# A layer's prologue with its loads in another order and its first projections on half the tokens

## The chip, the cores and the metric

The kernel runs on one core of a Trainium2 chip. The metric is the device time of one execution in microseconds; the times shown are of three runs. Beside them stands one profiled execution with its trace, in which every instruction of every engine has a start and a duration.

Engines are named as in the trace: PE (TensorE) with its weight loads PEld, DVE (VectorE), ACT (ScalarE), POOL (GpSimd), and SP, whose queue SPq issues all the DMA loads.

## What is computed

One layer of a flow-matching backbone, over 1024 latent tokens and 256 context tokens of width 1024. The part that the change touches is the beginning:

```python
m_lat = jnp.split(jax.nn.silu(c) @ w_mod + b_mod, 6, axis=-1)
h_lat = modulate(rms_norm(x_lat, norm_mix_pre), m_lat[0], m_lat[1])   # h * (1 + scale) + shift
q, k, v, r, lr, z, xbc, dt_raw = jnp.split(h_lat @ w_in, PROJ_SPLITS, axis=-1)
```

Behind it come the convolution of `xbc`, two bidirectional scans (gated linear attention and a state-space scan), the output projection and a SwiGLU block. They are the same before and after.

## The kernel before

Products are made in three fp16 parts: `split_w` makes of a weight block a high half on ACT (line 213) and a lower half on DVE (line 214), `mod_split` does the same for activations (lines 381 to 383), and `mm3` issues high times high, high times low and low times high (lines 219 to 221).

The first stage makes three 128-column blocks of the projection (`m` = 4, 5, 0, the ones that feed the convolution) for all latent tokens. The tokens are two halves of 512, the contraction has eight steps `k` of 128 channels, so there are 3 x 2 x 8 products of three matmuls. Their six accumulators `accs` fill the six PSUM buffers of the tag `ps` while the stage lasts. Two more PSUM buffers, tag `pf` (`psum_f`), serve whatever runs beside.

The stage needs

- x in eight tiles of 128 tokens (`load_x(t)`, t = 2 to 9, 512 KB each, line 363). `norms` squares and sums a pair of tiles (one on ACT, line 374, one on DVE, line 372), makes the reciprocal root (`rstd_act`, lines 194 to 199) and scales both tiles on DVE (line 377). `x_T(k, g, pool)` transposes channel block k of the four tiles of half g on PE (line 413) and copies the result out of PSUM, on ACT for even k and DVE for odd k (line 414).
- shift and scale of each channel. `mod_load(j)` loads two pieces of 256 columns of w_mod, 1 MB each (line 332; `wm`, four buffers), piece 1 for the scale and piece 0 for the shift; together they serve k = 2j and 2j + 1. `mod_mm` multiplies them with the condition on PE (line 340) and copies the result (ACT, line 343); `mod_fin` turns it into columns (PE, line 350) and makes `a8` and `b8` on DVE (lines 355 to 358), with the help of `vcol`, the small vectors that `vec_cols` transposes (lines 178 to 183).
- the weight blocks (`stage_w`, 512 KB each, line 208).

`split_x(k, i, eng)` applies `a8` and `b8` to half i of step k: on DVE (`hf`, line 381), high half on ACT (line 382), lower half on `eng` (line 383; V is DVE, G is POOL). `proj0(k, ms, halves)` issues the matmuls.

What sets the order: the loads go out on SP in the order of the program text, and a load can be held on its queue until an earlier one has landed. `vq` holds nine small loads of vectors (lines 391 and 392; 0.5 to 27 KB), which `vnext` issues one after the other between the big ones. The instructions of the compute engines are put in order when the kernel is built, by a planner that goes by program order and by when it expects operands to be ready; at run time each engine takes its own list strictly in that order. Where the text says `keep_in_program_order`, the planner doesn't move an instruction. Waits between engines are semaphores that are derived from the tiles.

In the kernel before, all eight x tiles are loaded first, with one small vector between two tiles from x5 on; then w_mod's first group with the remaining vectors, three weight blocks, and w_mod's second group. All four `norms` and the transposes stand ahead of `mod_mm(0)`, and each `proj0` handles both halves of the tokens.

Of the kernel before, what the change touches and what calls it, by code (L numbers as in the profile page):

```python
# [16 lines left out]
P = 128  # L17
D = 1024
KT = D // P
# [12 lines left out]
O_Q, O_K, O_V, O_R, O_LR, O_Z, O_X, O_DT = 0, 256, 512, 1024, 1536, 1568, 2080, 2848  # L32
# [12 lines left out]
def dit_layer_kernel(  # L45
# [8 lines left out]
    V, S, G, PE = nc.vector, nc.scalar, nc.gpsimd, nc.tensor  # L54
# [20 lines left out]
    def psum(shape=(P, 512), dtype=F32, name="ps"):  # L75
        return pp.tile(list(shape), dtype, tag="ps", bufs=6, name=name)
# [129 lines left out]
    def stage_w(src, nk, ncol, name):  # L206
        st = wp.tile([P, nk, ncol], F32, tag="wst", bufs=3, name=f"st_{name}")
        nc.sync.dma_start(st, src.rearrange("(k p) n -> p k n", p=P))
        return st
# [117 lines left out]
    def mod_load(j, between=lambda: None):  # L327
        for piece in (1, 0):
            wm = tmp0.tile([P, KT, 256], F32, tag="wm", bufs=4, name=f"wm{piece}_{j}")
            c0 = piece * D + j * 256  # L330
            between()
            nc.sync.dma_start(wm, w_mod[:, c0:c0 + 256].rearrange("(k p) n -> p k n", p=P))
            wms[j, piece] = wm

    def mod_mm(j, piece):
        wm = wms.pop((j, piece))
        ps = psum_f()
        for kk in range(2):
            for q in range(4):
                PE.matmul(ps[32 * q:32 * q + 32, :256], sc32[:, 4 * kk + q, :], wm[:, 4 * kk + q, :],  # L340
                          start=(kk == 0), stop=(kk == 1))
        mr = tmp0.tile([P, 256], F32, tag="mr", bufs=2, name="mr")
        tc.keep_in_program_order(S.copy(mr, ps[:, :256]))
        pms[j, piece] = mr

    def mod_fin(j, piece):
        mr = pms.pop((j, piece))
        ps = psum_f()
        for i in range(2):
            PE.matmul(ps[:, 2 * i:2 * i + 2], mr[:, i * P:(i + 1) * P], sel, start=True, stop=True)  # L350
        for i in range(2):
            k = 2 * j + i
            if piece:
                t = sm.tile([P, 2], F32, tag="mt", name="mt")
                V.tensor_scalar(t, ps[:, 2 * i:2 * i + 2], vc("bm", 8 + k), 1.0, ADD, ADD)
                V.tensor_scalar(a8[:, k, :], t, vc("gp", k), SH, MUL, MUL)
            else:
                V.tensor_scalar(b8[:, k, :], ps[:, 2 * i:2 * i + 2], vc("bm", k), SH, ADD, MUL)
# [34 lines left out]
    def vnext(n=1):  # L393
        for _ in range(n):
            if vq:
                vq.pop(0)()

    xl = {}
    for t in range(2, 10):
        if t > 4:  # L400
            vnext()
        xl[t] = load_x(t)
    mod_load(0, vnext)
    vnext(9)
    wst = {m: stage_w(w_in[:, O_X + m * P:O_X + (m + 1) * P], KT, P, f"x{m}") for m in (4, 5, 0)}
    mod_load(1)
    xT = [ar.tile([P, T], F32, tag="oS" if k < 4 else "oG", bufs=4, name=f"xT{k}") for k in range(KT)]

    def x_T(k, g, pool):
        ps = pool()  # L410
        for i in range(4):
            t = 2 + 4 * g + i
            PE.transpose(ps[:, i * P:(i + 1) * P], xl[t][:, k * P:(k + 1) * P], ident)
        (V.tensor_copy if k % 2 else S.copy)(xT[k][:, g * 512:g * 512 + 512], ps)

    def norms(ts, dve=()):
        norm_x([xl[t] for t in ts], dve)

    norms((2, 3), (1,))
    norms((4, 5), (1,))  # L420
    norms((6, 7), (1,))
    norms((8, 9), (1,))
    for k in range(KT):
        x_T(k, 0, psum)
    x_T(0, 1, psum)
    x_T(1, 1, psum)
    mod_mm(0, 1)
    vec_cols()
    mod_mm(0, 0)
    mod_fin(0, 1)  # L430
    mod_fin(0, 0)
    wx = {}
    accs = {(m, i): psum(name=f"cx{m}_{i}") for m in (4, 5, 0) for i in range(2)}

    def proj0(k, ms, halves=(0, 1)):
        for m in ms:
# [5 lines left out]
    def split_x(k, i, eng):  # L442
        o = slice(i * 512, i * 512 + 512)
        mod_split(hl[k][:, :, o], xT[k][:, o], k, 0, 512, eng)

    split_x(0, 0, V)
    wx[4] = split_w(wst[4], KT, P, "x4")
    split_x(0, 1, V)
    wx[5] = split_w(wst[5], KT, P, "x5")
    split_x(1, 0, G)  # L450
    wx[0] = split_w(wst[0], KT, P, "x0")
    split_x(1, 1, G)
    proj0(0, (4,))
    for k in range(2, KT):
        x_T(k, 1, psum_f)
    proj0(0, (5, 0))
    for j in range(4):
        if j < 2:
            mod_load(j + 2)
        if j == 2:  # L460
            xc_ = [load_x(0), load_x(1)]
            norm_x(xc_)
        for k in (2 * j, 2 * j + 1):
            for i in range(2):
                if j:
                    split_x(k, i, G if k % 2 else V)
        if j:
            proj0(2 * j, (4, 5, 0))
        if j < 3:
            for piece in (1, 0):  # L470
                mod_mm(j + 1, piece)
            proj0(2 * j + 1, (4,))
            for piece in (1, 0):
                mod_fin(j + 1, piece)
            proj0(2 * j + 1, (5, 0))
        else:
            proj0(2 * j + 1, (4, 5, 0))
    xin = {}
# [1450 lines left out]
```

## Time and profile before

| | |
|---|---|
| median of three runs | 1233.98 us (1229.95 to 1235.22) |
| profiled execution | 1230.18 us |
| its span in the trace | 1228.5 us |
| PE busy | 1169.6 us, 95% |
| DVE busy | 885.4 us, 72% |
| ACT busy | 603.9 us, 49% |
| POOL busy | 109.8 us, 9% |
| moved by DMA | 140.16 MB, 114 GB/s over the span |

A busy engine is one with an instruction in flight; matmuls overlap in the pipeline, so a matmul that lasts 0.38 us in a row may be followed by the next one 0.22 us later. Idle time of an engine is put down to the event that ended it. All times are counted from the start of the span.

### The profile page before, as it was taken

The page shows a single profiled execution, that of the slowest core. Times are in us where ns is not written, and L with a number is a line of the kernel's source. Part 1 is how long each engine was busy: PE and PEld are TensorE (multiplying, and loading weights), DVE is VectorE, ACT ScalarE, POOL GpSimd, SP SyncE. Part 2 cuts the span into 40 slices and gives each one's busy share as a digit, 9 for nine tenths or more (in the row PEclk, how much of TensorE's full clock was granted, in tenths as well). Part 3 has the DMA queues.
Part 4 walks back from the last instruction along what each step waited for, and adds up shares of the span by engine and source line. Part 5 has one row for each costly group of instructions (what it writes and reads, how often), then busy time and mean ns, then how long its engine had stood idle before and what let it go on. Part 6 is the DMA issues. An engine that isn't in the chain of part 4 may idle for free.

```text
span 1228.5 us, 20954 instructions
## 1 busy us (share of the span) xinstructions
PE 1169.6 (95%) x8336; PEld 662.1 (54%) x8336; DVE 885.4 (72%) x1605; ACT 603.9 (49%) x1233; POOL 109.8 (9%) x144
## 2 busy tenths in 40 slices
PE   4999999999999899999979999999999999999997
PEld 3465664767877588645434444444444444444444
DVE  7677896668478885966698677888987549654447
ACT  5447534555485564556673344455544434343423
POOL 0220042142300000100000000000000002200011
PEclk9999999999999999999989999999999999999999
DMA  9711101011210442566103234556553136310425
GB/s 308 232 36 52 52 19 52 18 35 46 71 36 3 146 165 71 180 208 230 52 24 119 64 112 146 175 185 223 188 173 120 53 104 205 126 71 33 148 82 202
DMA packets 90751, 140.16 MB, mean 114 GB/s; under 512 B 7592, under 2 KB 61597, under 8 KB 90653
## 3 DMA queue, kind: packets, MB, share of 16 engines
q1 hardware_dynamic: 90653, 138.82, 34.5%
q8 instruction: 65, 1.06, 0.4%
q14 instruction: 33, 0.27, 0.1%
HBM read 117.31 MB, written 20.97 MB: 113 GB/s over the span
## 4 chain that ended last, share of the span: by engine, by line
PE 73%; DVE 14%; ACT 6%; DMA 3%; issue 2%; POOL 1%; SPq 1%; DVEq 0%; ACTq 0%; POOLq 0%
PE ps L219 15%; PE ps L221 15%; PE ps L220 15%; PE pf L219 6%; PE pf L221 6%; PE pf L220 6%; PE ps L1173 2%; DVE acc L505 1%; PE ps L859 1%; PE cx L221 1%; PE cx L219 1%; DVE T L1484 1%; PE cx L220 1%; PE ps L1285 1%; DMA x<-in_x_dram 1%
## 5 line engine op out<-in xcount | busy, mean ns | idle before, releaser
L219 PE MATMUL ps<-T,wS 128*128 128x512 f16 x264 | 101.1, 383 | 7.8 <-DVE u L1663 7.8
L221 PE MATMUL ps<-T,wS 128*128 128x512 f16 x264 | 101.1, 384 | 0.0
L220 PE MATMUL ps<-T,wS 128*128 128x512 f16 x264 | 101.1, 383 | 0.0
L1771 DVE TENSOR_TENSOR ah<-hid,ah 128x512 f16<-128x512 f32 x66 | 50.4, 764 | 54.3 <-ACT ah L1770 54.3
L1546 ACT ACTIVATE wS<-S 128x512 f16<-128x512 f32 x88 | 54.3, 627 | 71.4 <-PE ps L221 25.0
L1770 ACT CAST ah<-hid 128x512 f16<-128x512 f32 x66 | 40.5, 618 | 84.6 <-PE ps L221 46.5
L1547 DVE SCALAR_TENSOR_TENSOR wS<-S,wS 128x512 f16<-128x512 f32 x88 | 59.6, 685 | 17.6 <-ACT wS L1546 17.3
L1547 DVE SCALAR_TENSOR_TENSOR wA<-wst,wA 128x512 f16<-128x512 f32 x66 | 45.3, 688 | 35.5 <-ACT wA L1546 35.4
L1546 ACT ACTIVATE wA<-wst 128x512 f16<-128x512 f32 x66 | 41.5, 629 | 55.7 <-PE ps L221 34.0
L1801 POOL TENSOR_TENSOR hid<-hid,hid 128x512 f32<-128x512 f32 x11 | 17.1, 1552 | 543.9 <-DVE hid L1793 519.2
L220 PEld LDWEIGHTS <-wS 128*128 128x128 f16 x352 | 34.6, 98 | 50.6 <-issue 10.1
L221 PEld LDWEIGHTS <-wS 128*128 128x128 f16 x352 | 34.7, 98 | 42.4 <-issue 1.3
L219 PEld LDWEIGHTS <-wS 128*128 128x128 f16 x352 | 34.6, 98 | 42.3 <-issue 1.4
L219 PEld LDWEIGHTS <-hl 128*128 128x128 f16 x448 | 42.5, 97 | 8.2 <-issue 3.1
L220 PEld LDWEIGHTS <-hl 128*128 128x128 f16 x448 | 42.5, 98 | 6.4 <-issue 2.4
L221 PEld LDWEIGHTS <-hl 128*128 128x128 f16 x448 | 42.5, 98 | 4.7 <-issue 0.4
L220 PEld LDWEIGHTS <-wA 128*128 128x128 f16 x264 | 25.8, 98 | 33.1 <-issue 2.3
L219 PE MATMUL ps<-wo,oT 128*128 128x512 f16 x112 | 42.5, 379 | 0.4 <-ACT hf L1478 0.4
L220 PEld LDWEIGHTS <-ah 128*128 128x128 f16 x264 | 25.8, 98 | 31.4 <-issue 0.3
L219 PEld LDWEIGHTS <-ah 128*128 128x128 f16 x264 | 25.8, 98 | 31.2 <-issue 0.2
L221 PEld LDWEIGHTS <-ah 128*128 128x128 f16 x264 | 25.8, 98 | 31.2
L221 PEld LDWEIGHTS <-wA 128*128 128x128 f16 x264 | 25.8, 98 | 31.1
(547 smaller groups left out, 3465.9 us busy)
## 6 DMA issues: line engine op xcount, KB each, us to landing
wmst<-in_w_mod_dram SPq DMA_DIRECT2D x32, 512.0 KB, 4.1
wst<-in_w_gate_dram SPq DMA_DIRECT2D x26, 512.0 KB, 5.5
wst<-in_w_up_dram SPq DMA_DIRECT2D x26, 512.0 KB, 3.6
wdb<-in_w_down_dram SPq DMA_DIRECT2D x22, 512.0 KB, 5.8
x<-in_x_dram SPq DMA_DIRECT2D x16, 512.0 KB, 6.2
wm<-in_w_mod_dram SPq DMA_DIRECT2D x8, 1024.0 KB, 10.4
t32d<-wdt SPq DMA_DIRECT2D x11, 512.0 KB, 2.6
t14d<-wdt SPq DMA_DIRECT2D x11, 512.0 KB, 3.0
```

The lines of the kernel that those rows point to most:

```text
L219: PE.matmul(ps, lh, rh, start=start, stop=False, skip_group_check=on)
L220: PE.matmul(ps, lh, rl, start=False, stop=False, skip_group_check=on)
L221: PE.matmul(ps, ll, rh, start=False, stop=stop, skip_group_check=on)
L505: V.scalar_tensor_tensor(acr[:, r0:r1, q0:q1], xr[:, r0 + dr:r1 + dr, q0 + dc:q1 + dc], cw, acr[:, r0:r1, q0:q1], MUL, ADD)
L859: PE.matmul(ps[64 * d:64 * d + 64, :256], bmt[:, t, 64 * g:64 * g + 64], xw, start=True, stop=True)
L1173: PE.matmul(out_, gh[:, s, t, d], mask, start=(s == 0), stop=(s == 1))
L1285: PE.matmul(out_[hh][64 * b:64 * b + 64, ci, :], ek[hs, j0:j0 + 64], eq[hs, i0:i0 + 64], start=True, stop=True)
L1546: S.activation(w[:, 0], src, AF.Copy, scale=SW)
L1547: V.scalar_tensor_tensor(w[:, 1], src, SW, w[:, 0], MUL, SUB)
L1770: S.copy(dst[:, 0], src)
L1771: V.tensor_tensor(dst[:, 1], src, dst[:, 0], SUB)
L1801: G.tensor_tensor(hidf[fb][:, 0], hidf[fb][:, 0], hidf[fa][:, 0], SUB)
```

## The change

Loads: tiles x2 to x5 come first, with four small vectors behind x4 and four behind x5 and then the last one; then w_mod's first group; weight block 4; tiles x6 to x9; blocks 5 and 0; w_mod's second group. `vnext(4)` stands behind `load_x` instead of ahead of it, and `mod_load(0)` has no small loads between its pieces.

Work: only the norms and transposes of the first half stand ahead of `vec_cols`, `mod_mm(0)` and `mod_fin(0)`. The splits of half 0 for k = 0 and 1 and their projections with block 4 follow, then the norms of the other tiles, projections of half 0 with block 5, and step by step the second half: the transposes of k = 0 and 1 through `psum_f` instead of `psum`, their splits, and the rest of k = 0. The lower halves for k = 1, made on POOL before, are made on DVE. The matmuls of k = 1 that are done early are left out of the first pass of the loop over j. The accumulators are allocated half by half.

```diff
-    xl = {}
-    for t in range(2, 10):
-        if t > 4:
-            vnext()
+    xl, wst = {}, {}
+
+    def stage_x(m):
+        wst[m] = stage_w(w_in[:, O_X + m * P:O_X + (m + 1) * P], KT, P, f"x{m}")
+
+    for t in range(2, 6):
         xl[t] = load_x(t)
-    mod_load(0, vnext)
+        if t > 3:
+            vnext(4)
     vnext(9)
-    wst = {m: stage_w(w_in[:, O_X + m * P:O_X + (m + 1) * P], KT, P, f"x{m}") for m in (4, 5, 0)}
+    mod_load(0)
+    stage_x(4)
+    for t in range(6, 10):
+        xl[t] = load_x(t)
+    stage_x(5)
+    stage_x(0)
     mod_load(1)
...
     norms((2, 3), (1,))
     norms((4, 5), (1,))
-    norms((6, 7), (1,))
-    norms((8, 9), (1,))
     for k in range(KT):
         x_T(k, 0, psum)
-    x_T(0, 1, psum)
-    x_T(1, 1, psum)
-    mod_mm(0, 1)
     vec_cols()
-    mod_mm(0, 0)
-    mod_fin(0, 1)
-    mod_fin(0, 0)
+    for piece in (1, 0):
+        mod_mm(0, piece)
+    for piece in (1, 0):
+        mod_fin(0, piece)
     wx = {}
-    accs = {(m, i): psum(name=f"cx{m}_{i}") for m in (4, 5, 0) for i in range(2)}
+    accs = {(m, i): psum(name=f"cx{m}_{i}") for i in range(2) for m in (4, 5, 0)}
...
     split_x(0, 0, V)
     wx[4] = split_w(wst[4], KT, P, "x4")
-    split_x(0, 1, V)
+    split_x(1, 0, V)
+    norms((6, 7), (1,))
+    norms((8, 9), (1,))
+    proj0(0, (4,), (0,))
+    proj0(1, (4,), (0,))
     wx[5] = split_w(wst[5], KT, P, "x5")
-    split_x(1, 0, G)
+    for k in range(2):
+        x_T(k, 1, psum_f)
+        split_x(k, 1, V)
+    proj0(0, (5,), (0,))
+    proj0(1, (5,), (0,))
     wx[0] = split_w(wst[0], KT, P, "x0")
-    split_x(1, 1, G)
-    proj0(0, (4,))
+    proj0(0, (4, 5), (1,))
     for k in range(2, KT):
         x_T(k, 1, psum_f)
-    proj0(0, (5, 0))
+    proj0(0, (0,))
...
-            proj0(2 * j + 1, (4,))
+            proj0(2 * j + 1, (4,), (0, 1) if j else (1,))
...
-            proj0(2 * j + 1, (5, 0))
+            if j:
+                proj0(2 * j + 1, (5, 0))
+            else:
+                proj0(1, (5,), (1,))
+                proj0(1, (0,))
```

## Rows read from the trace of the kernel before

**Rows 1.** Stretches: us; PE, PEld, DVE, ACT, POOL busy; clock; DMA share; GB/s.

```profile
36.60:43.40 6.80, 6.80 (x59) 3.50 (x59) 3.43 (x12) 2.21 (x5) 0.00 (x0) 1.00 0.96 304
43.40:72.00 28.60, 28.60 (x188) 13.98 (x187) 16.41 (x36) 12.66 (x26) 7.31 (x6) 1.00 0.45 124
...
0.00:31.00 31.00, 15.03 (x98) 9.45 (x99) 24.70 (x97) 15.91 (x32) 1.55 (x12) 1.00 0.95 308
31.00:72.00 41.00, 40.61 (x273) 19.99 (x272) 24.64 (x51) 17.72 (x35) 11.45 (x8) 1.00 0.62 185
```

**Rows 2.** Landing times: x issued at 1.6, 3.4, 10.3; wm at 12.9; st_x at 17.0.

```profile
DMA to landing us min/median/max: 3.2/3.2/3.2
...
DMA to landing us min/median/max: 6.9/6.9/6.9
...
DMA to landing us min/median/max: 5.6/5.6/5.6
...
DMA to landing us min/median/max: 9.7/9.7/9.7
...
DMA to landing us min/median/max: 9.3/9.3/9.3
```

**Rows 3.** Chain that ended last: start, us, what.

```profile
16.12 5.32 DMA vs<-in_conv_w_dram
...
31.20 3.33 DVE w_x L214 x2
```

**Rows 4.** DVE in time order: start, us, engine, line, instruction, idle before.

```profile
70.54 0.75 DVE L500 TENSOR_SCALAR acc<-xin,cwcol 128x1024 f32<-128x1024 f32 x1 [4.14 <-ACT xin L482]
```

**Rows 5.** All engines in time order, second w_mod group, and the first hf.

```profile
27.00 1.90 DVE L381 TENSOR_SCALAR hf<-xT,a,b 128x512 f32<-128x512 f32 x4
...
37.95 1.07 PE L340 MATMUL pf<-wm,sc 128*32 128x256 f32 x16
...
40.58 0.35 DVE L355 TENSOR_SCALAR mt<-pf,vcol 128x2 f32<-128x2 f32 x2 [3.37 <-PE pf L350]
...
41.36 1.45 DVE L381 TENSOR_SCALAR hf<-xT,a,b 128x512 f32<-128x512 f32 x3
```

**Rows 6.** PE in time order: second-half transposes, first projection, projections from k = 2.

```profile
26.59 1.99 PE L413 MATMUL pf<-ident,x 128*128 128x128 f32 x12
...
29.38 0.89 PE L219 MATMUL cx<-hl,w_x 128*128 128x512 f16 x2 [0.80 <-ACT hl L382]
...
43.44 0.59 PE L219 MATMUL cx<-hl,w_x 128*128 128x512 f16 x2
```

**Rows 7.** DVE by line, 0 to 41.3 us (busy us, mean ns), and in time order.

```profile
L377 DVE TENSOR_SCALAR x<-x,ry_x 128x1024 f32<-128x1024 f32 x8 | 5.7, 748 | 0.1
L372 DVE SCALAR_TENSOR_TENSOR jk<-x 128x1024 f16<-128x1024 f32 x4 | 4.9, 1221 | 2.6 <-DMA x<-in_x_dram 2.6
...
L414 DVE COPY xT<-ps 128x512 f32<-128x512 f32 x5 | 3.4, 684 | 0.5 <-PE ps L413 0.5
...
L383 DVE TENSOR_TENSOR hl<-hf,hl 128x512 f16<-128x512 f32 x2 | 1.3, 684 | 0.0
...
8.30 0.15 DVE L198 TENSOR_TENSOR rt_x<-rt_x,rv_x 128x2 f32<-128x2 f32 x1
...
11.50 0.16 DVE L199 SCALAR_TENSOR_TENSOR ry_x<-rt_x,ry_x 128x2 f32<-128x2 f32 x1
```

**Rows 8.** Tiles w_x and hl: duration ns min/median/max of lower halves.

```profile
L214 DVE SCALAR_TENSOR_TENSOR w_x<-st_x,w_x x3: 1217/1226/2178, 28.9 to 32.3; 128x1024 f16<-128x1024 f32 x3
...
L383 POOL TENSOR_TENSOR hl<-hf,hl x3: 1357/2042/2136, 31.4 to 43.7; 128x512 f16<-128x512 f32 x3
```

**Rows 9.** Later: the stretch with a lower clock, PE ahead of it.

```profile
118.47:125.30 6.83, 6.83 (x23) 3.82 (x23) 3.15 (x8) 5.00 (x14) 0.00 (x0) 0.50 0.02 5
...
114.56 0.38 PE L220 MATMUL pf<-hl,w_x 128*128 128x512 f16 x1
117.80 0.42 PE L574 MATMUL ps<-av,trs 128*128 128x80 f32 x2 [2.87 <-DVE av L748]
```

## The prediction

> **What bounds the kernel now.** I read the page first: its own span is 1228.5 us and PE is busy for 95% of it, so what can be won is PE's idle time, some 59 us. The table of stretches [rows 1] shows how much of that lies in this prologue: PE is busy for 15.0 of the first 31 us and for 40.6 of the next 41. The change works on the 31 us; from 31 us on the first stage (three 128-column blocks of the input projection over all 1024 tokens) is limited by PE itself.
>
> Next the DMA queue in order of time with the landings [rows 2]. The data that stage one needs first is 4 MB of x, 2 MB of w_mod, 1.5 MB of w_in and another 2 MB of w_mod, and from 1.6 us on the stream hardly pauses. Tile x2 lands at 1.6 + 3.2 = 4.8 us, x5 at 3.4 + 6.9 = 10.3, x9 at 10.3 + 5.6 = 15.9, the second piece of w_mod's first columns at 12.9 + 9.7 = 22.6, the second w_in block at 17.0 + 9.3 = 26.3. A later issue is held by an earlier landing: x9 went out at 10.3, just as x5, eight issues before it, had landed. So the prologue is a race between a stream of about 305 GB/s [rows 1] and the chain that eats it.
>
> Last the chain of waits and PE's own rows [rows 3]. It goes through the last small load (the convolution weights, issued at 16.12, on the chain until 21.44), the scaling of the last two x tiles, their transposes, the first w_mod products and scales, the modulated activations, and two lower halves of weights on DVE that end at 34.5. The first projection of an input whose scales come from the second group of w_mod columns, k = 2, starts at 43.44 [rows 6]. I use that instant as the ruler: from there on PE runs without a gap to 72.0, where the stage is all but over [rows 1], and behind it DVE's convolution taps wait for the stage's last evacuation (4.1 us idle until 70.54) [rows 4]. Whatever moves 43.44 moves the end about one to one.
>
> **The change part by part.**
>
> *The loads.* No byte is added or removed, only the order differs. The four first tiles land as now, about 10.3, with the same bytes ahead of them. The small vectors no longer alternate with tiles x6 to x9 but sit around x5, and all nine precede w_mod. As an issue follows the landing of the one eight before it, w_mod's first piece goes out at about 10, when the small loads behind x4 are in, and finds an emptied stream: from x2 (landed 3.2 us after its issue, of which about 1.4 is its transfer, a quarter of the 5.6 from x5 to x9) an empty stream needs 1.8 us to start, so with x5 in at 10.3 a hole of about 1.6 us opens (0 if the vectors land early; 3 if the last is as slow as the convolution weights now). Present rates, from the landings: 6.7 us for 2 MB of w_mod (15.9 to 22.6), 1.85 for a w_in block (22.6 to 26.3 for two), 1.4 for an x tile (10.3 to 15.9 for four) [rows 2]. So w_mod's first columns land at 11.9 + 6.7 = 18.6 instead of 22.6, w_in block 4 at 20.4, x7 at 23.2, x9 at 26.0 instead of 15.9, two more w_in blocks by 29.7, the next 2 MB of w_mod by 36.4. Today that last one is in at about 34.9 by the same arithmetic (26.3 + 1.9 + 6.7), so hidden behind PE, whose product with it starts at 37.95 [rows 5].
>
> *The first half, early.* The vectors' transposes no longer hang on a load queued behind w_mod. After w_mod's landing come product, copy, scale product and two DVE steps. In group two today this is 37.95 to 41.36, 3.4 us [rows 5], of which some 0.6 is projection work in between. So the first activations are formed from about 21.4 instead of 27.0 [rows 5], and PE's first projection stands at 22.5 instead of 29.4 [rows 6]. This is the gain that the change is able to make: about 6 us, on half the tokens.
>
> *What PE can do with it.* Up to 31 us there are 12 matmuls of half 0 (k = 0, 1 for blocks 4 and 5) that the code puts ahead. Two of them that lie together last 0.59 us of which one alone is 0.38 [rows 6, 9], so each adds 0.21 to 0.22; 12 are 2.6 us. Against them stands what PE does today before 31 and can't then: three groups of second-half transposes (12 in 1.99 us, so 0.6 to 0.66 a group [rows 6]), of which one or two now fit. PE's work between 31 us and the ruler today: 33 projection matmuls 7.1, three groups of transposes 1.9, two w_mod products 2.1, and their scale products, which I put at 0.8 to 1.0 as the DVE step at 40.58 waited for them and the product ended at 39.0 [rows 5]: together 11.9 to 12.1 of the 12.4 us. After: 24 matmuls 5.2, six to seven groups of transposes 3.6 to 4.2, the same 3.0, together 11.8 to 12.2, or 11.2 if block 0's first half gets in too. So the work that can be pulled forward is nearly paid back by transposes pushed behind: a gain of 0 to 1.3 us, and I take 0.8.
>
> *DVE.* It has slack today: it is busy for 3.4 of the 6.8 us before the ruler [rows 1] and waits 3.4 us ahead of the second group's scales [rows 5]. In the new order it must, after 21.4 us, do two lots of norms (in each a square 1.22, two scalings 0.75 each, four rstd steps 0.6: 6.6 us), three lower weight halves (1.23 each [rows 8], 3.7), four hf (0.48 [rows 5], 1.9) and four lower activation halves (0.68, all of them on DVE now: 2.7), and four copies of transposes (0.68: 2.7), 17.6 us [rows 7]. That ends at 39.0 if dense, just ahead of the second group's scales (36.4 + 2.6 to 3.4). The two halves taken from POOL cost 1.4 us of DVE, but of that some comes back: one lower weight half took 2.18 instead of 1.22 us while POOL worked on its 2.04 us halves [rows 8]. In sum 0.4, covered if DVE stays dense.
>
> *Small edits.* The order of the dictionary of accumulators and the other PSUM pool for two transpose groups move no data; the second pool has two buffers, emptied every 0.6 to 0.7 us, within the transpose price above (0 to 1 us; I take 0). Fewer projection matmuls stand between the second group's products and scales: 0.6 us less cover for the copy between them, included at 0.3.
>
> *Sum.* Ruler: 43.4 - 0.8 + 0.3 = 42.9; shift -0.5 us, with ends of -2 and +1.5 from the hole, DVE and the transposes. On the profiled execution's 1230.2 us this gives 1229.7. The median of the runs is 1234.0, the profiled one being near the lowest, so on the median **1233.5 us**.
>
> **A rule against it.** The granted clock falls later in this trace behind a long wait of PE: after 2.87 us of waiting at 117.80, with nothing new issued since 114.56, the stretch from 118.47 to 125.30 has a granted clock of 0.50, the 1.2 GHz level, while the prologue's stretches are all at 1.00 [rows 1, 9]. The Trainium skill, "TensorE: Matmul & The Clock Gate", section "HAM oscillation — how this bites in real kernels", says the same as a warning: matmuls in short batches with load waits between them start each batch cold. By that rule every batch of half 0 would start slow; the rows show the prologue's short waits at 1.00 and the long one followed by 0.50. The first rival has the price.
>
> **The rivals.**
>
> *The clock falls in the new gap (slower).* Between half 0's matmuls and the second half's transposes PE waits for x8 and x9 (landed 26.0, scaled about 30): two or three separated bits of work in 25 to 30 us. If PE stands still for 2.9 us there, the following 6.8 us run at half speed, which is 3.4 us lost. With -0.5 that is +2.9: 1236.9. It decides from a standstill like that of the row on; the prologue as it is leaves PE idle for 16.0 of its 31 us and is still at 1.00 [rows 1]. A stretch half as long again would give +4.6, 1238.6.
>
> *DVE takes the late tiles first (slower).* Engines take instructions in a fixed order, and DVE has already been seen holding a ready rstd step for 3 us behind a square that waited for its tile (8.30 to 11.50) [rows 7]. If the square of x9 is placed ahead of the first activations, these wait until 26.0 + 1.2; of the 17.6 us only the first lot of norms (3.3) and that square are then behind, 13.1 remain, which end at 40.3 dense and some 43 with the waits of a chain that has lost its lead; scales, hf and cast of k = 2 (1.8) come after: the ruler at 42 to 45, +1 on the mean and +2 at the end, 1235 to 1236.
>
> *The whole gain (faster).* If DVE and PE are fed so well that only w_mod's second group decides, the ruler is 36.4 + 3.4 + 0.5 + 0.6 (first hf and cast) = 40.9, or 39.3 without the hole: -2.5 to -4, 1230 to 1231.5. Against it stand the PE work after 31, 11.2 us at least, and DVE's 17.6.
>
> *It does nothing:* if the planner keeps an equivalent order, 1234; this is in the forecast's range.
>
> **How the numbers follow.** Forecast 0.55 (1233.5, own range 1231.5 to 1235.5), clock 0.16, DVE 0.12, whole gain 0.12, and 0.05 for a different order far behind the prologue, either sign. No mechanism here reaches 0.5% (6.2 us, about what a measurement of this kernel tells from no change); it takes one of them and the spread of the runs, 1229.95 to 1235.22. I give faster 0.11, within 0.5% 0.78, slower 0.11. The range goes from the whole gain less the runs' spread below, 1227, to a cold stretch with late DVE, 1240.
>
> **What would show it.** Right: w_mod's first columns landed at 18 to 19, first projection matmul at 22 to 23, x9 scaled at about 30, DVE busy nearly all the time from 21 to 39, k = 2 starting at 42 to 44, and the stage's end shifted by as much. Wrong: a granted clock of 0.5 before 40 us (first rival); squares of late x tiles ahead of the first hf on DVE (second); k = 2 by 40 (third); a stage's end that moves and a span that doesn't, or the reverse, for then the ruler was a bad one.

## The result and the profile after

| | before | after |
|---|---|---|
| median of six runs each | 1232.26 us (1229.95 to 1235.22) | 1239.11 us (1236.94 to 1240.31) |
| ratio, 95% interval | | 1.0051 [1.0036, 1.0066] |
| profiled execution | 1230.18 us | 1239.13 us |
| its span | 1228.5 us | 1237.4 us |
| PE busy | 1169.6 us | 1178.0 us |
| first convolution tap on DVE | 70.54 us | 76.64 us |

The forecast was no change; the kernel became about half a per cent slower. The first convolution tap is the prediction's stage end [rows 4]. Here is its row in the kernel after, on DVE in time order (start, us, engine, line, instruction, idle before):

```profile
76.64 0.75 DVE L515 TENSOR_SCALAR acc<-xin,cwcol 128x1024 f32<-128x1024 f32 x1 [4.14 <-ACT xin L497]
```

The wait ahead of it is the same 4.14 us; it all comes 6.10 us later. Row by row, DVE then stays 6.1 us behind the trace of the kernel before up to about 320 us, so this much was lost ahead of the tap. For the rest of the 8.9 us between the spans see the last section.

The stretches of the kernel after that answer to [rows 1] (us; PE, PEld, DVE, ACT, POOL busy; clock; DMA share; GB/s):

```profile
25.20:31.00 5.80, 3.40 (x9) 1.02 (x8) 5.41 (x15) 4.75 (x11) 0.00 (x0) 0.50 1.15 321
31.00:36.10 5.10, 4.19 (x13) 1.56 (x11) 4.29 (x8) 0.96 (x2) 0.00 (x0) 0.50 1.09 348
36.10:38.85 2.75, 2.74 (x13) 2.46 (x14) 1.93 (x5) 1.59 (x3) 0.00 (x0) 0.50 1.09 349
38.85:42.90 4.05, 4.05 (x25) 2.39 (x23) 2.54 (x4) 1.21 (x3) 0.00 (x0) 1.00 0.60 211
```

Two things are to be seen. The granted clock is at 0.50, the 1.2 GHz level, for 13.65 us, from 25.20 to 38.85; in the kernel before it was at 1.00 there. And PE is dense only from 36.1 on, while DVE is busy for 5.4 of the 5.8 us from 25.2 on: the work of the second half arrives late, and from DVE.

What DVE did with those microseconds (kernel after, DVE in time order; L214 are lower weight halves, L372 squares, L197 to L199 steps of the reciprocal root, L377 the scaling of two x tiles):

```profile
22.34 1.22 DVE L214 SCALAR_TENSOR_TENSOR w_x<-st_x,w_x 128x1024 f16<-128x1024 f32 x1
23.48 0.34 DVE L358 TENSOR_SCALAR b<-pf,vcol 128x2 f32<-128x2 f32 x2
23.73 1.00 DVE L381 TENSOR_SCALAR hf<-xT,a,b 128x512 f32<-128x512 f32 x2
24.96 1.29 DVE L383 TENSOR_TENSOR hl<-hf,hl 128x512 f16<-128x512 f32 x2 [0.23 <-ACT hl L382]
26.17 1.22 DVE L372 SCALAR_TENSOR_TENSOR jk<-x 128x1024 f16<-128x1024 f32 x1
...
27.58 1.22 DVE L372 SCALAR_TENSOR_TENSOR jk<-x 128x1024 f16<-128x1024 f32 x1
...
29.55 1.42 DVE L377 TENSOR_SCALAR x<-x,ry_x 128x1024 f32<-128x1024 f32 x2
30.89 0.15 DVE L197 SCALAR_TENSOR_TENSOR rt_x<-ry_x 128x2 f32<-128x2 f32 x1
30.95 1.22 DVE L214 SCALAR_TENSOR_TENSOR w_x<-st_x,w_x 128x1024 f16<-128x1024 f32 x1
32.09 0.15 DVE L198 TENSOR_TENSOR rt_x<-rt_x,rv_x 128x2 f32<-128x2 f32 x1
32.16 1.22 DVE L214 SCALAR_TENSOR_TENSOR w_x<-st_x,w_x 128x1024 f16<-128x1024 f32 x1
33.30 0.16 DVE L199 SCALAR_TENSOR_TENSOR ry_x<-rt_x,ry_x 128x2 f32<-128x2 f32 x1
33.49 1.42 DVE L377 TENSOR_SCALAR x<-x,ry_x 128x1024 f32<-128x1024 f32 x2
```

A weight half of 1.22 us stands ahead of the shifts of the first activations, and two more stand between three steps of 0.15 us that make the reciprocal root of x8 and x9. The first half's activations begin at 23.73 (27.00 before [rows 5]); x8 and x9 are scaled at 34.90. None of the late squares waits for a transfer.

The chain of waits of the kernel after shows what the two halves cost (start, us, what):

```profile
30.97 0.07 DVE rt_x L197
31.04 0.07 DVE w_x L214
31.11 0.98 issue
32.09 0.15 DVE rt_x L198
32.25 0.07 DVE w_x L214
32.31 0.98 issue
33.30 0.17 DVE ry_x L199
```

The chain goes from one small step to the next through 1.05 us of weight half each time ("issue": DVE waits for nothing, it works through its list). Then ACT and PE in time order, a block each:

```profile
24.31 1.14 ACT L382 CAST hl<-hf 128x512 f16<-128x512 f32 x2 [2.27 <-DVE hf L381]
25.35 1.05 ACT L374 ACTIVATE jk<-x 128x1024 f16<-128x1024 f32 x1
```

```profile
24.98 0.40 PE L219 MATMUL cx<-hl,w_x 128*128 128x512 f16 x1 [2.08 <-ACT hl L382]
...
30.06 0.61 PE L219 MATMUL cx<-hl,w_x 128*128 128x512 f16 x1 [2.07 <-ACT w_x L213]
...
34.30 1.35 PE L421 MATMUL pf<-ident,x 128*128 128x128 f32 x4 [0.18 <-DVE x L377]
36.11 2.89 PE L421 MATMUL pf<-ident,x 128*128 128x128 f32 x12 [0.46 <-ACT xT L422]
...
42.97 1.29 PE L340 MATMUL pf<-wm,sc 128*32 128x256 f32 x20
...
48.88 0.82 PE L219 MATMUL cx<-hl,w_x 128*128 128x512 f16 x3
```

ACT waits 2.27 us for the first activations and only then squares x6. PE has two waits of about 2.1 us, the second-half transposes follow the scaled tiles at once, and the second w_mod group's products come from 42.97 on (the second of them at 37.95 before [rows 5]). The projection of k = 2, the last row, starts at 48.88 instead of 43.44 [rows 6].

### The profile page after: what moved, and what is told of

It is laid out like the page before. It is cut to its first block, busy times and chain, and to the rows that moved or that the text cites. A ratio compares the mean times of both kernels' runs of the same rounds, so it can differ in the third digit from the quotient of the medians.

```text
span 1237.4 us, 20956 instructions
## 1 busy us (share of the span) xinstructions
PE 1178.0 (95%) x8336; PEld 670.4 (54%) x8336; DVE 884.1 (71%) x1607; ACT 605.2 (49%) x1233; POOL 117.5 (9%) x142
## 3 DMA queue, kind: packets, MB, share of 16 engines
q1 hardware_dynamic: 90653, 138.82, 34.3%
## 4 chain that ended last, share of the span: by engine, by line
PE 75%; DVE 12%; ACT 6%; DMA 2%; issue 2%; POOL 1%; SPq 0%; DVEq 0%; ACTq 0%; POOLq 0%
PE ps L219 15%; PE ps L221 15%; PE ps L220 15%; PE pf L219 6%; PE pf L221 6%; PE pf L220 6%; PE ps L1188 2%; DVE acc L520 1%; PE ps L1300 1%; PE ps L874 1%; PE cx L219 1%; DVE T L1499 1%; PE cx L220 1%; PE cx L221 1%; PE pf L340 1%
## 5 line engine op out<-in xcount | busy, mean ns | idle before, releaser
L1816 POOL TENSOR_TENSOR hid<-hid,hid 128x512 f32<-128x512 f32 x11 | 27.5, 2512 | 532.4 <-DVE hid L1808 514.0
L1562 DVE SCALAR_TENSOR_TENSOR wA<-wst,wA 128x512 f16<-128x512 f32 x66 | 45.4, 689 | 35.2 <-ACT wA L1561 35.1
L220 PEld LDWEIGHTS <-wA 128*128 128x128 f16 x264 | 25.8, 98 | 32.5 <-issue 1.7
```

The costliest lines, as they stand in the source:

```text
L220: PE.matmul(ps, lh, rl, start=False, stop=False, skip_group_check=on)
L1562: V.scalar_tensor_tensor(w[:, 1], src, SW, w[:, 0], MUL, SUB)
L1816: G.tensor_tensor(hidf[fb][:, 0], hidf[fb][:, 0], hidf[fa][:, 0], SUB)
```

## The experiments

The theory after this reading has three causes of the 6.1 us: the order on DVE ahead of the last tiles' scaling, the half clock, and whatever is left by the late tiles. The rivals are that one of them alone is the cause. As span and time also carry falls of the clock far behind the prologue, the first tap is the ruler (before: 70.54, and 70.25 in a second execution).

**Each part alone.** One kernel has the new order of loads with the old work:

```diff
-    for t in range(2, 10):
...
+    for t in range(2, 6):
         xl[t] = load_x(t)
+        if t > 3:
+            vnext(4)
     vnext(9)
+    mod_load(0)
+    stage_x(4)
+    for t in range(6, 10):
+        xl[t] = load_x(t)
...
```

> The new order of the loads, with the whole order of the work as before. The mark is the start of the first convolution tap on DVE, which waits for the first stage's last evacuation: 70.5 us before, 76.6 after the change (+6.1). Theory A, the loads: the late tiles, landing at 25.6 instead of 15.9, are what the stage waits for, so this kernel loses as much as the whole change or more, because here even the scales of w_mod stand behind the late squares on ACT: mark 75 to 79. Theory B, the order of the work: with the old work the mark stays within 1.5 us of before, 70 to 72. Theory C, the clock: the mark is late only if the granted clock falls to 0.5 in the stretch from 20 to 40 us, and then by half of PE's busy time in that stretch.

The other is the kernel after with the old order of loads:

```diff
-    for t in range(2, 6):
+    for t in range(2, 10):
+        if t > 4:
+            vnext()
         xl[t] = load_x(t)
...
+    mod_load(0, vnext)
```

> The old order of the loads, with the whole new order of the work. Theory A, the loads: all tiles are in by 16 us, w_mod's first columns at 22.6 as before, so the mark comes back to 69.5 to 72. Theory B, the order of the work: the squares of the four later tiles stand behind the casts of the first half on ACT, so they can't start before about 27 us although the tiles are there; the scaling of the last tiles ends at 35 to 37 and the mark is at 75 to 78. Theory C, the clock: late only with a granted clock of 0.5 before 40 us.

First tap at 78.44 and at 79.03, 7.9 and 8.5 us later than before, so by this mark, in one execution each, either part alone costs more than both. The first lies in the range of its theory A; the second goes the way of its theory B and beyond its range. With the new loads, in the old order of work, the first activations have to wait for all eight tiles (37.02); the clock is at half for 17.07 us (stretch of that kernel, columns as above):

```profile
22.37:39.44 17.07, 7.49 (x31) 5.82 (x32) 13.17 (x34) 6.99 (x17) 0.00 (x0) 0.50 1.11 341
```

Half of PE's busy time in it, which theory C named as the price, is 3.7 us, less than half of the 7.9.

With the old loads, x8 and x9 are in early but are scaled only at 37.71. Of the four late squares, x6 and x8 are made on ACT and x7 and x9 on DVE: the two on ACT stand behind the casts of the first half, the one of x8 at 31.36, and weight halves stand in between on DVE. This is ACT's row for x8 in that kernel:

```profile
31.36 1.04 ACT L374 ACTIVATE jk<-x 128x1024 f16<-128x1024 f32 x1
```

So the order of the work costs even when the tiles are there, and neither part can be blamed alone.

**The clock: extra transposes on PE.** The kernel after, with 24 transposes of a tile into an accumulator that is not yet in use, 12 ahead of the first projection and 12 behind it:

```diff
+    def warm(n):
+        for _ in range(n):
+            tc.keep_in_program_order(PE.transpose(accs[0, 1][:, :P], xl[5][:, :P], ident))
+
+    warm(12)
     split_x(0, 0, V)
...
     proj0(1, (4,), (0,))
+    warm(12)
```

> The changed kernel with 24 more transposes on PE, 12 behind the first scale products (PE stood still there for 2.1 us) and 12 behind the six matmuls of block 4 on the first half (2.1 us again); their results are overwritten and nothing waits for them but PE itself. Theory C, the clock: the granted clock stays at 1.00 from 25 to 39 us and the mark comes back by 4 to 6 us, to 71 to 73. Theory A or B, the second half is late: the clock stays up too, but PE waits for the tiles scaled at 34.9 all the same; what is won is the half speed from 34.3 to 38.9, at most 2.3 us: mark 74.4 to 76.5.

First tap at 77.39, which neither theory had. The clock fell all the same, only later: 0.50 from 30.79 to 41.03, so that 6.75 us of it lay behind the scaling of x8 and x9 (34.28) where it was 3.95 us in the kernel after. What counted was where the half-clock stretch ended, not how long it was (10.24 us here, 13.65 there).

**The order on DVE.** The lower halves of blocks 5 and 0 may be issued only behind the scaling of x8 and x9 (called the pins below):

```diff
+    late = norms((8, 9), (1,))
...
+    with tc.issue_after(late.ins):
+        wx[5] = split_w(wst[5], KT, P, "x5")
...
+    with tc.issue_after(late.ins):
+        wx[0] = split_w(wst[0], KT, P, "x0")
```

> The changed kernel with the lower halves of weight blocks 5 and 0 pinned behind the scaling of tiles 8 and 9 on DVE; in the changed kernel they (2 x 1.22 us) stood between the small steps of the reciprocal root, and the scaling ended at 34.9. Theory B, the order on DVE: the scaling ends 2.4 us earlier, about 32.5, the second half's transposes and splits follow, and the mark comes back by 1.5 to 2.4 us, to 74.2 to 75.1. Theory C, the clock: PE has the same work at half speed; with the block-5 matmuls now later too the mark stays at 76 to 77.5.

> The changed kernel with the lower halves of weight blocks 5 and 0 pinned behind the scaling of the last x tiles, once more and timed. Theory A (VectorE's order costs 2.6 us of the shift): first tap at 73 to 75 and a ratio to the kernel before of 1.0030 (1.002 to 1.004), against 1.0051 for the changed kernel. Theory B (the gain of the single look was its clock): first tap at 76 to 77, ratio 1.0045 or more.

First tap at 74.01, and 73.81 in the second execution, ratio 1.0038 [1.0024, 1.0052]: both inside what theory A of the second text expected, and a little more gain than theory B of the first (74.2 to 75.1, the scaling at about 32.5). On DVE (first execution, in time order) the root's steps now follow each other and the halves come behind:

```profile
29.81 0.15 DVE L197 SCALAR_TENSOR_TENSOR rt_x<-ry_x 128x2 f32<-128x2 f32 x1
30.00 0.16 DVE L198 TENSOR_TENSOR rt_x<-rt_x,rv_x 128x2 f32<-128x2 f32 x1
30.20 0.16 DVE L199 SCALAR_TENSOR_TENSOR ry_x<-rt_x,ry_x 128x2 f32<-128x2 f32 x1
30.39 1.42 DVE L377 TENSOR_SCALAR x<-x,ry_x 128x1024 f32<-128x1024 f32 x2
31.73 1.22 DVE L214 SCALAR_TENSOR_TENSOR w_x<-st_x,w_x 128x1024 f16<-128x1024 f32 x1
```

x8 and x9 are scaled at 31.81: 9.15 us behind the first activations (22.66) instead of 11.17, so the two halves cost 2.0 us. In the first execution the half clock was as long as in the kernel after (22.94 to 36.59); in the second it came in two stretches, 23.00 to 26.42 and 29.83 to 36.66.

**Both together.** The same pins and 14 + 20 extra transposes:

> The kernel of e4 (lower halves of blocks 5 and 0 behind the scaling of tiles 8 and 9; mark 74.0) with 34 extra transposes on PE, 14 behind the first scale products and 20 behind the six matmuls of block 4, so that PE isn't idle while it waits for casts and tiles. Theory C, the clock has a share of its own: in e4 PE was dense from 31.2 us, and 5.4 us of that were still at half speed; with the clock at 1.00 there the mark falls by 2.0 to 2.7 us, to 71.3 to 72.0. Theory B alone, the order on DVE: PE has slack in that stretch and the mark stays at 73.3 to 74.3. If the clock still falls before 37 us, the run tells nothing of its share.

> The kernel of the run with the weight halves pinned and TensorE kept going, once more and timed. Theory A (whatever moves the first convolution tap moves the end one to one): first tap at 72.2 as in its first run, 1.7 us behind the kernel before, so a ratio of 1.0014 (1.0005 to 1.0025) against 1.0051 for the changed kernel. Theory B (the changed kernel's time has a part that has nothing to do with the prologue): a ratio of 1.003 or more at the same first tap.

In the first execution the clock didn't fall, with the tap at 72.21, 0.2 us behind the clock theory's 71.3 to 72.0 and 1.8 us ahead of the pins alone; x8 and x9 were scaled at 31.87 as with the pins alone, so these 1.8 us are the clock's. In the second one of the same kernel the clock did fall (stretches of the first, then of the second):

```profile
25.20:38.85 13.65, 10.97 (x73) 7.54 (x72) 12.45 (x26) 7.59 (x16) 0.00 (x0) 1.00 1.09 336
```

```profile
22.45:25.86 3.41, 3.41 (x15) 2.52 (x14) 3.18 (x7) 2.19 (x4) 0.00 (x0) 0.50 1.11 345
25.86:32.69 6.83, 5.07 (x34) 3.38 (x32) 6.33 (x17) 4.56 (x9) 0.00 (x0) 1.00 1.12 333
32.69:36.10 3.41, 3.31 (x10) 1.82 (x11) 3.41 (x6) 1.12 (x3) 0.00 (x0) 0.50 1.09 348
```

The tap was at 73.64, not 72.2, and the ratio 1.0029 [1.0016, 1.0042]. The tap that both theories counted on was missed, and with it theory A's 1.0014. This tap, 3.1 to 3.4 us behind the kernel before, would give about 1.0026, near the measured ratio. But it belongs to the slowest of the ten runs (1238.99 us, against a median of 1237.43), so theory B's part of the time that has nothing to do with the prologue is not excluded. Extra work on PE makes the half clock shorter there (0, 6.8 and 10.2 us in these two executions and the one with 24 transposes, against 10.2 to 17.1 us without) and does not exclude it.

**The first activations earlier.** Block 4's lower half stands behind the shifts instead of ahead:

```diff
+    with tc.issue_after(shift.ins):
+        wx[4] = split_w(wst[4], KT, P, "x4")
```

> The changed kernel with block 4's lower half pinned behind b8 on DVE, where it stood ahead of it for 1.2 us while the first activations waited. The first hf comes 1 to 1.3 us earlier (22.5 to 22.8 instead of 23.7). If the first half isn't what the stage waits for (the second half and PE's total are), the mark stays at 76.6 within 0.5 us. If the early start of the first half counts one to one, as the prediction's hopeful case has it, the mark falls to 75.3 to 75.7.

The first activations begin at 22.87 instead of 23.73, of which only some 0.5 us is the change's: from DVE's step of line 355 to them it is 1.44 us here and 1.91 there. x8 and x9 are scaled at 34.93 as in the kernel after (34.90): the weight half only changes its place in the same full list of DVE. The half clock lasted until 41.45, and the tap stood at 77.93, outside both expectations; by the line further down, the longer half clock makes up 1.0 of the 1.3 us by which it is later than in the kernel after. That an earlier first half is worth nothing by itself is shown for the scaling of the late tiles, not for the tap.

**The late squares.** The norms of x6 to x9 ahead of the first splits in the text, with pins, first with the 34 extra transposes and then without:

```diff
+    norms((6, 7), (1,))
+    late = norms((8, 9), (1,))
     split_x(0, 0, V)
...
-    norms((6, 7), (1,))
-    late = norms((8, 9), (1,))
     proj0(0, (4,), (0,))
```

> The changed kernel with the lower halves of weight blocks 5 and 0 pinned behind the scaling of the last x tiles and with 34 extra transposes that keep TensorE going (as in the run of both together, whose first convolution tap stood at 72.2 us), and in addition the norms of tiles x6 to x9 stand in the text ahead of the first splits, so that their squares on ScalarE are no longer fixed behind the casts of the first activations. Theory A (what is left of the shift, 1.7 us, is the late tiles being handled late: ScalarE squares x6 3.7 us after it landed): x8 and x9 scaled at 29 to 30.5 instead of 31.9, first tap at 70.3 to 71.3, the time within 0.1% of the kernel before. Theory B (what is left is the work itself, PE's dense stretch after the tiles and the second w_mod group, and the order of the norms does not decide): tiles scaled earlier but the first tap stays at 71.8 to 72.7. Granted clock at 1.00 up to 100 us in both.

> The changed kernel with the lower halves of weight blocks 5 and 0 pinned behind the scaling of the last x tiles, and the norms of tiles x6 to x9 in the text ahead of the first splits; no extra transposes (in the earlier run with them, 20 of them at half clock stood in the way from 30.0 to 34.3 us, so that run could not tell). Theory A (late tiles handled late are the rest of the shift): x8 and x9 scaled at 30.0 to 31.3, first convolution tap 0.5 to 1.8 us ahead of the 74.0 us of the run with the pin alone, at like clock. Theory B (the load order sets the rest: x9 lands at 25.6 and needs its 5 to 6 us of square, root and scaling however the text stands): x8 and x9 scaled at 31 to 32, first tap within 0.5 us of 74.0 at like clock, and TensorE dense only from 32 us.

The first of them went against both theories: the tap at 75.12, ratio 1.0061 [1.0042, 1.008]. The clock was at half from 27.09 to 33.92, and 20 extra transposes ran in it (PE in time order):

```profile
30.04 4.25 PE L454 MATMUL cx<-ident,x 128*128 128x128 f32 x20
```

They ended at 34.3, 3 us after x8 and x9 were scaled (31.24), so the experiment measured its own filler. Without it the tap is at 75.04 and the ratio 1.0037 [1.0024, 1.005]. DVE of that kernel, in time order:

```profile
26.73 1.42 DVE L377 TENSOR_SCALAR x<-x,ry_x 128x1024 f32<-128x1024 f32 x2
28.06 1.22 DVE L372 SCALAR_TENSOR_TENSOR jk<-x 128x1024 f16<-128x1024 f32 x1
...
30.53 1.42 DVE L377 TENSOR_SCALAR x<-x,ry_x 128x1024 f32<-128x1024 f32 x2
```

The scaling of x6 and x7 begins 1.8 us earlier than with the pins alone (28.48 there), but the square of x9 now stands behind them and x9 is done at 31.95: 8.48 us behind the first activations (23.47 here) against 9.15. So this order is worth 0.7 us, in both runs alike. It decides little. Of the two theories the second is nearer, as x8 and x9 came at 31 to 32; the tap itself tells neither, since the first activations came late in this execution and the clock was at half until 38.58, 2 us longer than with the pins alone.

**Both kernels once more.**

> The kernel before, unchanged, for a second trace. In the traces of the changed kernel and of e1 to e4 the granted clock falls once more at 490 to 496 us, for 7 to 10 us, and the shift against before grows there by 2.7 to 4.4 us; the first trace of before has no such stretch. If the stretch is chance, it may show here too, with a span of 1231 to 1234; if the changed prologue brings it about, this trace has none and a span of 1228 to 1230. The mark is at 70.5 within 0.3 in both cases.

> The changed kernel once more, one look. Theory A (a stretch at half clock ahead of 40 us belongs to this order of the work): a stretch of at least 6.8 us at 0.50 between 20 and 40 us again, first convolution tap at 75.5 to 77.5. Theory B (the fall came by chance, as those near 118 and 490 us do): clock at 1.00 up to 100 us and the first tap at 74.5 to 75.2.

Before: first tap at 70.25, no fall of the clock in the prologue, 1230.9 us. The fall near 490 us is there, so the changed prologue is not needed for it; the span is 1229.2 us and not the 1231 to 1234 expected with it, as the fall near 118 us is missing. After: first tap at 74.67 instead of 76.64, time 1238.65 us. Its stretches, then the start of k = 2 on PE and the tap:

```profile
22.95:33.20 10.25, 6.66 (x16) 2.12 (x15) 9.59 (x21) 6.01 (x12) 0.00 (x0) 0.50 1.12 334
33.20:74.67 41.47, 40.29 (x272) 20.55 (x273) 23.71 (x53) 16.64 (x33) 8.68 (x6) 1.00 0.59 174
```

```profile
46.92 0.82 PE L219 MATMUL cx<-hl,w_x 128*128 128x512 f16 x3
```

```profile
74.67 0.75 DVE L515 TENSOR_SCALAR acc<-xin,cwcol 128x1024 f32<-128x1024 f32 x1 [4.13 <-ACT xin L497]
```

The half clock is there again, as theory A has it, but ends at 33.20, before x8 and x9 are scaled (33.97), and the tap stands where theory B wanted it. Both are half right: the fall belongs to this order (it is in all six profiled executions with it and no extra transposes: after twice, the pins twice, the early shifts, the early squares), and when it ends differs from one execution to the next.

**The vectors alone.** The kernel before, with two small vectors ahead of each of x5 to x9 and none between and behind the w_mod pieces:

```diff
-            vnext()
+            vnext(2)
         xl[t] = load_x(t)
-    mod_load(0, vnext)
-    vnext(9)
+    mod_load(0)
```

> The kernel before with one part of the idea alone: the small vectors go out two at a time between tiles x5 to x9, all ahead of w_mod, and nothing else moves. The transposes of the vectors no longer wait for a load behind w_mod (they ran at 24.0), so a8 and b8 depend on w_mod's landing at 22.6 alone. Theory: the first hf moves from 27.0 to 25.5 to 26.3 and the mark from 70.5 to 69.2 to 70.3, a ratio of 0.999, not to be told from 1. Rival: the small loads hold up the tiles behind them, x9 lands later than 15.9 by 0.5 to 1 us, and the mark stays at 70.5 or comes later.

> The kernel before with two small vectors ahead of each of the tiles x5 to x9 and none between and behind the w_mod pieces, nothing else; a second set of timings. Theory A (the 1.2 us by which the first convolution tap came earlier in its first run is real and carries to the end): ratio 0.9990 (0.998 to 1.000) and first tap at 69.0 to 69.7. Theory B (chance): ratio 1.000 to 1.001.

First execution: tap at 69.34, 1.2 us earlier than before, ratio 0.9984 [0.9972, 0.9995]; the first activations at 26.97, so the expected 25.5 to 26.3 was missed. Second: the tap at 71.16, ratio 0.9994 [0.9985, 1.0003]. The stretch in which they differ, first and second execution:

```profile
22.58:32.82 10.24, 8.48 (x59) 4.97 (x59) 8.77 (x19) 6.86 (x11) 0.19 (x1) 1.00 1.07 302
```

```profile
22.58:32.82 10.24, 9.73 (x51) 6.05 (x46) 7.30 (x18) 5.59 (x9) 0.00 (x0) 0.50 1.15 318
```

With the old order of the work and of the big loads the clock can fall in the prologue too, in one of four executions (two of the kernel before, two here). A gain of about 0.1% is likely and not shown: the first interval leaves out 1, the second does not, and of the second text's two theories the ratio lies in A's range and the tap (69.0 to 69.7) missed it. Nothing else that was tried was as fast as the kernel before.

## Why the prediction was wrong

**The account that the runs give.** In the nine profiled executions with the new loads and the new work (the one whose extra transposes stood in the way is left out; it lies 2.4 us above the line given below) the tap follows from two numbers: when x8 and x9 are scaled, and how long the half clock lasts beyond that. The lag between scaling and tap is:

| kernel | x8, x9 scaled | half clock beyond | lag to the tap |
|---|---|---|---|
| pins and extra transposes, first | 31.87 | 0 | 40.34 |
| after, second execution | 33.97 | 0 | 40.70 |
| pins and extra transposes, second | 31.73 | 3.41 | 41.91 |
| after, first execution | 34.90 | 3.95 | 41.74 |
| pins, first | 31.81 | 4.78 | 42.20 |
| pins, second | 31.37 | 5.29 | 42.44 |
| early squares and pins | 31.95 | 6.63 | 43.09 |
| early shifts | 34.93 | 6.52 | 43.00 |
| after with 24 transposes | 34.28 | 6.75 | 43.11 |

A straight line through these is 40.5 us plus 0.38 us for each microsecond of half clock, all nine within 0.3 us. It describes them and is no proof, but the runs that moved one term alone lie on it: the pins move the first column, the clock the second. If the fit may choose how much a microsecond of later scaling costs, it comes out at 1.00 us. With x9 scaled at 30.0, as the prediction had it, and without half clock beyond, the line gives a tap at 70.5, where it was before; no run was there, as the nine lie between 31.4 and 34.9. The kernel with the old loads and the new work (scaled at 37.71, 4.42 us of half clock beyond, lag 41.32) lies 0.9 us below the line. So the first execution's 6.1 us are 34.90 - 30.0 = 4.9 from the scaling and 0.38 x 3.95 = 1.5 from the clock, less 0.3 that the line leaves; the second's 4.1 us are 33.97 - 30.0 = 4.0 from the scaling and nothing from a half clock beyond it.

**Right.**
- *The loads.* By the landing times of the trace after, w_mod's first group landed at 18.6 (forecast 18.6), x9 at 25.6 (26.0), the second group at 35.1 (36.4), and nobody waits for the last.
- *The way from the tiles to the ruler.* From x9's scaling to k = 2 the forecast's two instants lie 12.9 us apart (30.0 to 42.9); in the second execution, at full clock, it took 12.95 (33.97 to 46.92). The prediction never worked this difference out by itself, so that it fits so closely is in part luck.
- *The ruler.* k = 2 moved by 5.4, the tap by 6.1 us, the time by 6.9 us between the medians. In the second execution they are 3.5 and 4.1 us: from k = 2 to the tap it takes 27.10 us before and 27.76 and 27.75 after, a difference of 0.65 us whose cause stays open. For the pins alone the taps (3.3 to 3.8 us later) give 1.0027 to 1.0031 and the runs 1.0038 [1.0024, 1.0052].

**Wrong: "x9 scaled at about 30".** It had no working of its own in the prediction; it was taken as its landing and some four microseconds. In the sum it stands behind the term of -0.8: PE's 11.8 to 12.2 us of work were to run without a gap from 31 us to the ruler, but a part of them, the second half's transposes, needs x6 to x9 scaled. Measured: scaled at 34.90 and 33.97, with PE at the transposes of x8 and x9 from 34.30 and 33.36 on. From the first activations at 21.4 the prediction had 8.6 us to it; the runs show 11.2 in both executions, and 9.15 once the two weight halves are pinned behind. So 2.0 of the missing 4 to 5 us are two weight halves between steps of 0.15 us that the prediction had in its DVE sum but not in an order. Another 1.4 to 2.3 us are the first activations themselves (22.79 and 23.73 for 21.4): a third weight half of 1.22 us stood ahead of the shifts, and in the first execution PE's slow start came on top (last paragraphs of this section). Moving that weight half back alone did not bring the scaling forward, as the late tiles are behind both. What is left, some 0.5 us, is about what squares ahead of the casts gave back (0.7). PE's first projection, forecast for 22.5, stood at 24.98 and 24.04.

**Wrong: DVE's sum as a test.** "17.6 us dense, ends at 39.0" asked whether DVE has enough time; it had (it was busy for 5.4, 4.3 and 1.9 us of the three half-clock stretches, 11.6 of 13.65 us, and waited 3.13 us ahead of the second group's scales) and the stage was late all the same, since PE can do little for the second half until the two last tiles are through (four transposes of x6 and x7 from 30.89 on). A sum over a window has no order in it. The rival on DVE looked at one bad order, squares ahead of the first activations; the opposite one happened, first-half work and weight halves ahead of the squares and roots.

**Too small: the clock.** The rival was named, with its sign, its wrong signal (a clock of 0.5 before 40 us) and a chance of 0.16. It was there in every execution of the new order without extra work, for 10.2 to 17.1 us, and not the 6.8 us that the later stretch before showed [rows 9]. The standstill of 2.9 us that was named as its condition did not come: a wait of 2.08 us ended just ahead of the fall at 25.20, and a second one of 2.07 us followed. The rule from the Trainium skill ("TensorE: Matmul & The Clock Gate", section "HAM oscillation — how this bites in real kernels") that was weighed against the change says that short batches of matmuls with load waits between them start each batch cold; this trace agrees with it in part, as the batches that begin at 24.98 and 30.06 ran at half clock, the first from 25.20 on, and the waits ahead of them, about 2.1 us each, were for high halves made on ACT and not for loads.

The price is less than the forecast's half of the stretch, since PE has slack ahead of the scaling: it was busy for 3.40 of the 5.80 us from 25.20 on. It is 0.38 us for each microsecond that lies beyond the scaling, 1.5 us in the first execution and none in the second.

**Missing: the slow start of the clock.** The two executions of the kernel after differ by 0.94 us already in the first activations (23.73 and 22.79). The profile's record of the clock begins at 18.37 us in the first and at 16.13 in the second, and the clock column gives 1.00 for what lies ahead of that, where nothing is recorded. The transposes on PE tell more (duration in ns, min/median/max; three rows of the kernel after, first execution, then one of the kernel before):

```profile
L421 PE MATMUL ps<-ident,x x27: 354/421/477, 12.4 to 18.2; 128*128 128x128 f32 x27
L421 PE MATMUL pf<-ident,x x16: 404/421/477, 34.3 to 38.6; 128*128 128x128 f32 x16
L421 PE MATMUL pf<-ident,x x13: 272/273/404, 38.6 to 41.9; 128*128 128x128 f32 x13
L413 PE MATMUL ps<-ident,x x9: 374/421/474, 13.8 to 15.9; 128*128 128x128 f32 x9
```

A transpose lasts 421 ns at a recorded 0.50 and 273 at 1.00, and the first ones last 421. So PE's first work, behind a wait of 9.43 us, ran at the half level as well, until about 18.4 us in the first execution and 16.1 in the second, and until about 16.1 in the kernel before. The prediction's "all at 1.00" [rows 1] is therefore right for the column, but not for what PE did ahead of that time. In the first execution the chain of waits to the first activations goes through these transposes, in the second through the landing of weight block 4 (a row of each chain: start, us, what):

```profile
12.39 6.73 PE ps L421 x32
```

```profile
10.60 9.69 DMA st_x<-in_w_in_dram
```

So of the 1.97 us between the two taps, 0.93 is mostly this slow start, which delays the scaling (PE itself began only 0.15 us later, 12.39 for 12.24), and 1.04 lies behind the scaling, with the half clock of 3.95 us and of none. The clock thus has a share in the first execution's 4.9 us too, beside the 1.5.

## What to carry to other kernels

When work is split so that one half can start early, follow the late half's own chain through every engine's list, one instruction after another, down to the smallest steps: a sum of busy time per engine says that it fits and not when it is done. A 0.15 us step that several engines wait for is worth pinning ahead of 1.2 us pieces that nobody needs yet; here that was worth 2.0 us. And batches of early matmuls with waits between them can meet a clock at half just ahead of the dense stretch that pays for it: here they did in every execution of the new order without extra work, though what sets off the fall was not shown.

## What the runs showed of the hardware

The clock's falls are not a property of the kernel alone. In the prologue, behind the slow start, the same kernel with pins and extra transposes had no fall in one execution and two stretches of 3.41 us at 0.50 in another; the kernel with the vectors earlier had none and then 10.24 us; the kernel after had 13.65 and 10.24 us. Further back there is a fall near 118 us, missing in the second execution of before, and one near 490 us, missing in the first of before and present in its second (485.25 to 492.08) and in the kernel after (492.83 to 503.07). In the first comparison of traces this last one is most of what the spans differ by beyond the 6.1 us. It is not the change's alone, as both executions with the vectors earlier have it too (483.74 to 493.98 and 486.79 to 497.03), and single spans of this kernel cannot be compared to better than some 3 us. A mark ahead of the first of these later falls can.

Over whole executions the mean granted clock was 0.979 to 0.982 in the six runs after and 0.983 to 0.990 in 21 runs of before that were timed beside the later experiments: at their middles, 0.9795 and 0.986, that is, as an estimate, 2 x 0.0205 x 1237 = 51 us against 2 x 0.014 x 1232 = 34 us at half clock. Of the 17 us more, the 10 to 14 us recorded in the prologue of the two executions after would be the largest part.
